# Making a modulation's sums for two channel tiles in a row, with a sixth slab buffer and the loads one slab further ahead

## The chip, the cores and the metric

The kernel runs on one core of one Trainium2 chip. The metric is the device time of one execution, in microseconds (us), as the median of several runs. Names used below: TensorE (PE) multiplies matrices and loads its weights (PEld), VectorE (DVE) and ScalarE (ACT) work on elements, GpSimd (POOL) does little here, and SyncE (SP) issues the transfers (DMA) from the device memory into the on-chip buffers. TensorE writes its results into banks of an accumulation memory, PSUM, from which VectorE and ScalarE read them.

## What is computed

One step of a backbone with one layer, for 128 context tokens and 256 latent tokens (384 in all), 2048 channels wide. The whole layer has two sub-layers, a mixer and a feed-forward part, each between two normalisations, and six vectors per condition that shift, scale and gate them. What the change touches is the first of these:

```
mod = silu(cond) @ w_ada + b_ada            # 6 vectors of 2048 channels, per condition
sh1, sc1, ga1, sh2, sc2, ga2 = split(mod, 6)
h = rmsnorm(x, norm_pre_mix) * (1.0 + sc1) + sh1
proj = h @ w_in                             # q, k, v, gates, low-rank factors, Fourier groups
```

There are two conditions, one for the context tokens and one for the latent ones. The vectors `sh1` and `sc1` come first, since nothing of the mixer can begin before h. The rest (attention with gates, a Fourier branch, their merge, the feed-forward part) follows and is not touched.

## The kernel before, in words

Everything is held with channels on the 128 partitions: x is 16 channel tiles of 128 channels by 384 tokens. Products in full precision are made of three passes over a high and a low half: a weight block is loaded (`raw`), ScalarE casts it to its high half (`whi`), VectorE subtracts to get the low half (`wlo`), and TensorE multiplies high by high, high by low and low by high.

The first stage is a loop over the 16 channel tiles, `for kb in range(KT)` at line 456. For tile kb it needs shift and scale for the 128 channels of that tile. These are a product of the two condition vectors with 2048 x 256 elements of the weights, kept as a "slab" of 2 MB: two buffers of 1 MB, loaded by `load_slab` (line 321). `gemv` (line 375) makes the sums: 16 matmuls over the 16 blocks of K, each with a stationary block of 32 columns, dealt out in turn to four groups of 32 partitions of the bank `pgm` (half `pgv`). The sums, spread over four groups, are copied by ScalarE (`ev`, line 490), transposed by TensorE into the other half (`pmod`, line 496), and reduced by VectorE (line 504), which then makes scale and shift (lines 507 and 511) and the modulated tile (line 513). ScalarE casts that to the high half of h (line 283), VectorE makes the low half (line 284).

In the same turn TensorE works on the tile before, kb-1: `vprod` (line 387) adds its part to all of v in six banks, in three passes of six matmuls, and `xprod` (line 411) makes two blocks of 128 columns in a single bank `px`, which VectorE adds up after each (line 409). In tiles 6, 10 and 14 a low-rank product (`lrprod`, line 421) comes in as well. For these products each tile loads a weight of 512 KB for v (`raw`, line 195) and a small one of 128 KB (`xraw`, line 331), each with two buffers; `split_w` (line 333) casts both, and the low halves are made by VectorE at the end of the turn, the large one at line 224, the small one at line 345.

The order on TensorE, ScalarE, VectorE and GpSimd is that of the program, written out by hand. In a plain turn TensorE does: the sums of kb; first xprod of kb-1; vprod pass 0; two transposes; second xprod; vprod pass 1; vprod pass 2. In tiles 1 and 2 (`wait`) a vprod pass and the first xprod come ahead of the sums. SyncE issues all transfers from one queue in the order of the program; an issue waits until its buffer is free. In turn kb it issues slab kb+1 (five half-slab buffers in all), the weight kb+1 and the small weight kb+1; in turn 4 five small loads follow (lines 362 to 366).

Of the kernel before, what the change touches and what calls it, by code (L numbers as in the profile page):

```python
# [11 lines left out]
F32 = mybir.dt.float32  # L12
# [8 lines left out]
P = 128  # L21
D = 2048
KT = D // P
# [73 lines left out]
def tile_step(ctx: ExitStack, tc: tile.TileContext, a, o):  # L97
    nc = tc.nc
    PE, ACT, DVE, POOL, SP = nc.tensor, nc.scalar, nc.vector, nc.gpsimd, nc.sync
# [9 lines left out]
    spad = const.tile([P, KT, 32], F32, name="spad")  # L109
# [5 lines left out]
    ident = const.tile([P, P], F32, name="ident")  # L115
# [23 lines left out]
    def halves(t):  # L139
        tl = [actp.tile([P, 8, T], F32, tag=f"{t}_{n}", name=f"{t}{n}") for n in ("hi", "lo")]  # L140
        return lambda k: tl[k // 8][:, k % 8, :], tl
# [48 lines left out]
    def load(raw=None):  # L190
        n, src = next(srcs, (0, None))
        if src is not None:
            if raw is None:
                raw = wp.tile([P, G], F32, tag="raw", name="raw", bufs=2)
            SP.dma_start(raw, src)
            raws.append((raw, n in folded))
# [85 lines left out]
    def split_act(hi, lo, src):  # L282
        ACT.copy(hi, src)
        DVE.tensor_sub(lo, src, hi.bitcast(F32))  # L284
# [31 lines left out]
    with ExitStack() as s:  # L316
        pa = s.enter_context(tc.tile_pool(name="pa", bufs=1))
        pb = s.enter_context(tc.tile_pool(name="pb", bufs=2))
        slabs = {}

        def load_slab(kb):
            slabs[kb] = [pb.tile([P, KT // 2, 256], F32, tag="slab", name="slab", bufs=5) for _ in range(2)]
            for n, sl in enumerate(slabs[kb]):
                SP.dma_start(sl, a["w_ada1"][kb, :, n * (KT // 2) : (n + 1) * (KT // 2), :])

# [2 lines left out]
        def load_w(kb):  # L328
            load()
            xraw[kb] = pb.tile([P, XU * P], F32, tag="xraw", name="xraw", bufs=2)  # L330
            SP.dma_start(xraw[kb], a["w_x"][kb])
# [17 lines left out]
        for q in range(4):  # L349
            SP.dma_start(  # L350
                xnt[q // 2][:, 4 * (q % 2) : 4 * (q % 2) + 4, :], a["xT"][:, 4 * q : 4 * q + 4, :],
            )
        load_slab(0)
        SP.dma_start(cols, a["b_ada"])
        SP.dma_start(norms, a["norms"])
        load_w(0)
        load_slab(1)
        load_w(1)
        wlr = pa.tile([P, KT, 32], F32, name="wlr")

        def load_later():
            SP.dma_start(wlr, a["w_lr"])
            SP.dma_start(coef[:, 0:2], a["consts"][:, C_COEF : C_COEF + 2])
            SP.dma_start(bgate, a["b_gate"])
            SP.dma_start(gnorm, a["gnorm"])
            SP.dma_start(selr, a["consts"][:, C_SELR : C_SELR + 64])
# [2 lines left out]
        pv = [psm.tile([P, 512], F32, tag="mm", name="pv") for _ in range(3)]  # L369
        pv += [pss.tile([P, 512], F32, tag="side", name="pv") for _ in range(3)]  # L370
        pgm = pss.tile([P, 512], F32, tag="side", name="pgm")
        pgv, pmod = pgm[:, 0:256], pgm[:, 256:512]
        px = pss.tile([P, T], F32, tag="side", name="px")

        def gemv(kb, ks=range(KT)):
            slab = slabs[kb]
            for k in ks:
                q = 32 * (k % 4)
                PE.matmul(  # L379
                    pgv[q : q + 32, :], spad[:, k, :], slab[k // (KT // 2)][:, k % (KT // 2), :],  # L380
                    start=k < 4, stop=k >= KT - 4,
                )

# [3 lines left out]
        def vprod(kb, w, parts, ts=range(3)):  # L387
            js = passes(w)
            tg = [(t, g) for t in ts for g in range(2)]
            if kb < KT - 1:  # L390
                order = [(j, t, g) for j in parts for t, g in tg]
            else:
                order = [(j, t, g) for t, g in tg for j in parts]
            for j, t, g in order:
                x_, w_ = js[j]
                PE.matmul(  # L396
                    pv[2 * t + g], hT[x_][:, kb, t * P : (t + 1) * P], w_[:, g * 512 : (g + 1) * 512],
                    start=kb == 0 and j == 0, stop=kb == KT - 1 and j == 2,
                )
# [11 lines left out]
        def xprod(u, kb, w):  # L411
            def mm():
                for j, (x_, w_) in enumerate(passes(w)):
                    PE.matmul(px, w_[:, u * P : (u + 1) * P], hT[x_][:, kb, :], start=j == 0, stop=j == 2)  # L414

            return mm, lambda dst=None: flush(xacc[u], kb == 0, dst)

        def lrprod(kb):
            def mm():
                for q in range(4):  # L420
                    PE.matmul(
                        px[32 * q : 32 * q + 32, :], wlr[:, kb + q, :], scr[:, (kb + q) % 8, :], start=True, stop=True,
                    )

            return mm, lambda dst=None: flush(lracc, kb == 0, dst)
# [20 lines left out]
        DVE.tensor_scalar_add(bsc1[:, 0, :], cols[:, 1, :], 1.0)  # L446
        DVE.tensor_scalar_add(bsc1[:, 1, :], cols[:, 4, :], 1.0)
        gemv(0, range(KT // 2, KT))
        ev = pb.tile([P, 256], F32, tag="ev", name="ev")
        ACT.copy(ev, pgv)  # L450
        for t in range(3):
            PE.matmul(px[:, t * P : (t + 1) * P], r0[:, t : t + 1].to_broadcast([P, P]), ident, start=True, stop=True)
        rstd = pa.tile([P, T], F32, name="rstdA")
# [1 line left out]
        prev = None  # L455
        for kb in range(KT):
            if kb and kb + 1 < KT:
                load_slab(kb + 1)
                load_w(kb + 1)
                if kb == 4:  # L460
                    load_later()

            wait = kb in (1, 2)
            if kb and not wait:
                gemv(kb)
            todo = []
            if kb > 4 and kb % 4 == 2:
                todo.append(lrprod(kb - 6))
            if kb:
                todo += [xprod(u, kb - 1, prev[1]) for u in range(XU)]  # L470
            todo += [None] * (4 - len(todo))
            flushes = [t[1] if t else lambda: None for t in todo]

            def pe_x(n):
                if todo[n]:
                    todo[n][0]()

            if wait:
                vprod(kb - 1, prev[0], (0,))
            pe_x(0)  # L480
            hf = scr[:, kb % 8, :]

            xr = hf if kb else qs[0]
            DVE.tensor_mul(xr, xn(kb), rstd if kb else px)
            flushes[0]()
            if wait:
                gemv(kb)
            if kb:
                ev = pb.tile([P, 256], F32, tag="ev", name="ev")
                ACT.copy(ev, pgv)  # L490
            lag = []
            new = split_w(kb, lag)
            if kb:
                vprod(kb - 1, prev[0], (1 if wait else 0,))
            for m in range(2):
                PE.transpose(pmod[:, m * P : (m + 1) * P], ev[:, m * P : (m + 1) * P], ident)
            if kb == 0:

                for _ in range(6):
                    PE.matmul(pv[5][:, 0:P], ones, ones, start=True, stop=True)  # L500
            pe_x(1)

            pm = pb.tile([P, 2, 2], F32, tag="pm", name="pm", bufs=2)
            DVE.tensor_reduce(
                pm, pmod.rearrange("p (m q r) -> p m r q", m=2, q=4)[:, :, 0:2, :], axis=mybir.AxisListType.X, op=ALU.add,
            )
            DVE.tensor_scalar(
                mods[:, 1, kb, :], pm[:, 1, :], bsc1[:, 0, kb : kb + 1], norms[:, 0, kb : kb + 1],
                op0=ALU.add, op1=ALU.mult,
            )  # L510
            DVE.tensor_scalar_add(mods[:, 0, kb, :], pm[:, 0, :], cols[:, 0, kb : kb + 1])
            for lo, hi, c in segs:
                DVE.tensor_scalar(
                    hf[:, lo:hi], xr[:, lo:hi], mods[:, 1, kb, c : c + 1], mods[:, 0, kb, c : c + 1],
                    op0=ALU.mult, op1=ALU.add,
                )
                if kb == 0:
                    ACT.activation(
                        hT[0][:, kb, lo:hi], xr[:, lo:hi], AF.Identity,
                        bias=mods[:, 0, kb, c : c + 1], scale=mods[:, 1, kb, c : c + 1],  # L520
                    )
            flushes[1]()
            if kb:
                split_act(hT[0][:, kb, :], hT[1][:, kb, :], hf)
            else:
                ACT.copy(rstd, px)
                DVE.tensor_sub(hT[1][:, kb, :], hf, hT[0][:, kb, :].bitcast(F32))
            if kb:
                if not wait:
                    vprod(kb - 1, prev[0], (1,))  # L530
                pe_x(2)
                flushes[2]()
            for sub in lag:
                sub()
            if kb:
                vprod(kb - 1, prev[0], (2,))
                pe_x(3)
                flushes[3]()
            prev = new
# [504 lines left out]
    mg32, _ = halves("B")  # L1044
    x1, x1t = halves("C")
    with ExitStack() as s:
# [49 lines left out]
        for i in range(KT):  # L1096
            p = psm.tile([P, T], F32, tag="mm", name="pmm")
            for g in range(2):
                n = 2 * i + g - 2 * KT
# [381 lines left out]
        n = 0  # L1481
# [100 lines left out]
        for kind, c, i in steps:  # L1582
# [8 lines left out]
            if kind == "D":  # L1591
                w = grab2()
                n, kh = i // 2, i % 2
                if kh == 0:
# [3 lines left out]
                    pool, tag = (pss, "side") if done % 2 or (c, n) == (NFC - 2, 3) else (psm, "mm")  # L1598
# [52 lines left out]
        n = d_order[-1]  # L1651
# [145 lines left out]
```

## Time and profile before

| | |
|---|---|
| median of 3 runs | 1960.13 us (1959.51 to 1961.31) |
| the profiled execution's own time | 1962.6 us |
| its span | 1960.3 us |
| PE busy | 1943.0 us (99%) |
| DVE busy | 1630.9 us (83%) |
| ACT busy | 908.6 us (46%) |
| first stage, tiles 0 to 15 | sums from 15.3 to 132.5 us, end at about 138 us |
| slab loads | 32 of 1 MB, 9.8 us from issue to landing in the median |

A row of a timeline has the start and the duration in us, the engine, the line, the operation, what is written from what, the form, and the count; in brackets stands how long the engine was idle before and what ended that. "SPq" rows are the issues of transfers, not the transfers. In a table by stretches each row gives a stretch in us, its length, then busy time and (number of instructions) of PE, PEld, DVE, ACT and POOL, the granted clock of TensorE as a share of full speed, the share of the DMA engines' time that was in use, and GB/s. A row of a tile gives the minimum, median and maximum duration in ns. Matmuls overlap one another, so a busy TensorE need not be at its peak: the distance from start to start tells what an instruction costs in a row of its kind.

### The profile page before, as it was taken

What the parts mean: (1) busy time and instruction counts of PE and PEld (TensorE: products, weight loads), DVE (VectorE), ACT (ScalarE), POOL (GpSimd) and SP (SyncE); (2) the same over time, 40 slices, a digit from 0 to 9 for tenths busy, and PEclk for the clock granted to TensorE, in tenths of its full rate; (3) what the DMA queues carried; (4) which work ended last, traced back from release to release, by engine and by line L of the source; (5) the groups of instructions that cost most, each with busy time, mean ns of one, the idle gap of its engine ahead of it and who ended that gap; (6) DMA issues with size and microseconds to landing.
All of it is one profiled execution on the core that took longest, in us unless ns stands there. A gap on an engine that the chain in (4) does not pass through costs nothing.

```text
span 1960.3 us, 27459 instructions
## 1 busy us (share of the span) xinstructions
PE 1943.0 (99%) x10544; PEld 1720.4 (88%) x10544; DVE 1630.9 (83%) x2091; ACT 908.6 (46%) x1281; POOL 32.2 (2%) x44
## 2 busy tenths in 40 slices
PE   8999999999999999999999999999999999999998
PEld 5679999999999999999988888888888888888886
DVE  5668788878767797977789998999898989887875
ACT  4233454544345654446455444444444444444444
POOL 0000000000000000004000000000000000000001
PEclk9999999999999999999999999999999999999999
DMA  9977677767755786755345445463536263626243
GB/s 389 373 259 268 220 257 238 233 218 246 246 189 158 224 268 217 233 183 206 111 148 172 161 133 170 140 196 121 193 123 208 94 213 108 202 74 193 74 157 134
DMA packets 189267, 380.05 MB, mean 194 GB/s; under 512 B 14029, under 2 KB 112525, under 8 KB 184785
## 3 DMA queue, kind: packets, MB, share of 16 engines
q1 hardware_dynamic: 188992, 377.92, 58.0%
q8 instruction: 82, 1.34, 0.3%
q14 instruction: 49, 0.39, 0.1%
q10 hardware_dynamic: 144, 0.39, 0.1%
HBM read 361.48 MB, written 16.78 MB: 193 GB/s over the span
## 4 chain that ended last, share of the span: by engine, by line
PE 87%; DMA 6%; issue 3%; DVE 3%; ACT 1%; POOL 0%; POOLq 0%; SPq 0%; ACTq 0%; DVEq 0%
PE pgu L1498 31%; PE pmm L257 30%; PE pdn L1498 16%; PE pv L396 2%; DMA slab<-in_w_ada 1%; PE pf L996 1%; DMA raw<-in_w_in 1%; PE pgm L379 1%; PE pmm L1252 1%; DVE wlo L224 1%; DVE adacc L572 1%; DMA raw<-in_w_out 1%; PE px L414 1%; PE ptr L1559 1%; ACT whi L223 1%
## 5 line engine op out<-in xcount | busy, mean ns | idle before, releaser
L257 PE MATMUL pmm<-A_hi,whi 128*128 128x384 f32 x1200 | 404.4, 337 | 0.0
L257 PE MATMUL pmm<-A_lo,whi 128*128 128x384 f32 x1200 | 401.5, 335 | 0.5 <-DVE A_lo L284 0.5
L257 PE MATMUL pmm<-A_hi,wlo 128*128 128x384 f32 x1200 | 401.4, 334 | 0.0
L1399 ACT CAST whi<-u 128x1024 fp32r<-128x1024 f32 x200 | 210.8, 1054 | 286.4 <-DVE u L1383 86.2
L223 ACT CAST whi<-raw 128x1024 fp32r<-128x1024 f32 x181 | 189.7, 1052 | 211.8 <-DMA raw<-in_w_gate 72.5
L1399 ACT CAST whi<-raw 128x1024 fp32r<-128x1024 f32 x175 | 184.3, 1053 | 197.8 <-PE pgu L1498 61.1
L224 DVE TENSOR_TENSOR wlo<-raw,whi 128x1024 fp32r<-128x1024 f32 x179 | 218.4, 1222 | 67.1 <-ACT whi L223 64.8
L1410 DVE TENSOR_TENSOR wlo<-u,whi 128x1024 fp32r<-128x1024 f32 x200 | 244.2, 1221 | 33.6 <-ACT whi L1399 18.4
L1498 PE MATMUL pgu<-whi,A_hi 128*128 128x512 f32 x640 | 250.0, 391 | 0.0
L1498 PE MATMUL pgu<-whi,A_lo 128*128 128x512 f32 x640 | 249.3, 389 | 0.0
L1410 DVE TENSOR_TENSOR wlo<-raw,whi 128x1024 fp32r<-128x1024 f32 x175 | 213.6, 1220 | 34.4 <-ACT whi L1399 25.1
L257 PEld LDWEIGHTS pmm<-A_hi,whi 128*128 128x128 f32 x1200 | 225.3, 188 | 2.9 <-issue 1.4
L257 PEld LDWEIGHTS pmm<-A_lo,whi 128*128 128x128 f32 x1200 | 225.4, 188 | 1.2 <-DVE A_lo L284 1.0
L257 PEld LDWEIGHTS pmm<-A_hi,wlo 128*128 128x128 f32 x1200 | 225.3, 188 | 0.0
L572 DVE SCALAR_TENSOR_TENSOR adacc<-adaw,spad,adacc 128x1024 f32<-128x1024 f32 x180 | 222.9, 1280 | 0.4
L1498 PE MATMUL pdn<-whi,hid_hi 128*128 128x512 f32 x480 | 186.9, 389 | 0.0
L1498 PE MATMUL pdn<-whi,hid_lo 128*128 128x512 f32 x480 | 186.8, 389 | 0.0
L1498 PE MATMUL pgu<-wlo,A_hi 128*128 128x512 f32 x640 | 184.2, 389 | 0.0
L1498 PEld LDWEIGHTS pgu<-whi,A_hi 128*128 128x128 f32 x640 | 120.1, 188 | 26.0 <-issue 0.8
L1498 PEld LDWEIGHTS pgu<-wlo,A_hi 128*128 128x128 f32 x640 | 120.2, 188 | 25.3
L1498 PEld LDWEIGHTS pgu<-whi,A_lo 128*128 128x128 f32 x640 | 120.2, 188 | 25.0
L1498 PE MATMUL pgu<-whi,S 128*128 128x512 f32 x480 | 131.1, 395 | 0.0
(369 smaller groups left out, 2759.2 us busy)
## 6 DMA issues: line engine op xcount, KB each, us to landing
adaw<-in_w_ada SPq DMA_DIRECT2D x96, 512.0 KB, 4.1
raw<-in_w_d SPq DMA_DIRECT2D x88, 512.0 KB, 3.7
slab<-in_w_ada SPq DMA_DIRECT2D x32, 1024.0 KB, 9.8
raw<-in_w_gate SPq DMA_DIRECT2D x64, 512.0 KB, 4.7
raw<-in_w_g SPq DMA_DIRECT2D x48, 512.0 KB, 3.3
raw<-in_w_u SPq DMA_DIRECT2D x48, 512.0 KB, 3.6
raw<-in_w_in SPq DMA_DIRECT2D x44, 512.0 KB, 4.4
u<-in_w_u SPq DMA_DIRECT2D x40, 512.0 KB, 4.8
```

What stands on the lines that cost most here:

```text
L223: ACT.copy(hi, raw)
L224: sub = lambda: eng.tensor_sub(lo, raw, hi.bitcast(F32))
L257: PE.matmul(dst, w[wi][:, k * n + n0 : k * n + n0 + P], x[xi][:, k0 + k, :], start=first and k == 0 and j == 0, stop=last and k == kts - 1 ...
L379: PE.matmul(pgv[q : q + 32, :], spad[:, k, :], slab[k // (KT // 2)][:, k % (KT // 2), :], start=k < 4, stop=k >= KT - 4,)
L396: PE.matmul(pv[2 * t + g], hT[x_][:, kb, t * P : (t + 1) * P], w_[:, g * 512 : (g + 1) * 512], start=kb == 0 and j == 0, stop=kb == KT - 1 ...
L414: PE.matmul(px, w_[:, u * P : (u + 1) * P], hT[x_][:, kb, :], start=j == 0, stop=j == 2)
L572: DVE.scalar_tensor_tensor(acc[:, c, :], w, spad[:, k, c : c + 1], acc[:, c, :], op0=ALU.mult, op1=ALU.add,)
L996: PE.matmul(pf[:, 0 : 2 * HT], w[0][:, c], x[k], start=k == 0, stop=False)
L1252: PE.matmul(hp[u], hw[u][j][:, ((k - 1) % 8) * P : ((k - 1) % 8 + 1) * P], h2[m][:, k - 1, :], start=k == 1 and j == m == 0, stop=k == KT ...
L1399: ACT.copy(hi, src)
L1410: DVE.tensor_sub(lo, src, hi.bitcast(F32))
L1498: PE.matmul(dst, stat[x_][m], mov(w[w_], m), start=first and w_ == m == x_ == 0, stop=last and w_ == m == 1,)
```

## The change

From the ninth tile on (kb = 8) the sums are made for two tiles in a row: in an even turn `gemv` runs for kb and for kb+1, the one into the first half of `pgm`, the other into the second; a single copy takes all 512 columns to `ev`, which now has one buffer of 512 columns instead of two of 256. In the odd turn there are no sums and no copy. The transposes of a tile go back into its own half of the bank. For that, slabs have six half-slab buffers, and the loads are further ahead: in turn 3 two slabs are issued, 4 and 5, the second after the weights of tile 4, and after that each turn kb issues slab kb+2 ahead of the weights of kb+1. The order of everything else is the same.

```diff
-            slabs[kb] = [pb.tile([P, KT // 2, 256], F32, tag="slab", name="slab", bufs=5) for _ in range(2)]
+            slabs[kb] = [pb.tile([P, KT // 2, 256], F32, tag="slab", name="slab", bufs=6) for _ in range(2)]
...
-        load_slab(0)
+        slab_order = iter(range(KT))
+
+        def next_slab():
+            kb = next(slab_order, None)
+            if kb is not None:
+                load_slab(kb)
+
+        next_slab()
...
-        load_slab(1)
+        next_slab()
...
-        pgv, pmod = pgm[:, 0:256], pgm[:, 256:512]
...
-        def gemv(kb, ks=range(KT)):
+        def gemv(kb, ks=range(KT), at=0):
...
-                    pgv[q : q + 32, :], spad[:, k, :], slab[k // (KT // 2)][:, k % (KT // 2), :],
+                    pgm[q : q + 32, at : at + 256], spad[:, k, :], slab[k // (KT // 2)][:, k % (KT // 2), :],
...
-        ev = pb.tile([P, 256], F32, tag="ev", name="ev")
-        ACT.copy(ev, pgv)
+        ev = pb.tile([P, 512], F32, tag="ev", name="ev", bufs=1)
+        ACT.copy(ev[:, 0:256], pgm[:, 0:256])
...
             if kb and kb + 1 < KT:
-                load_slab(kb + 1)
+                next_slab()
                 load_w(kb + 1)
+                if kb == 3:
+                    next_slab()
                 if kb == 4:
                     load_later()
...
-            if kb and not wait:
+
+            pair = kb >= 8
+            if pair and kb % 2 == 0:
+                for n in range(2):
+                    gemv(kb + n, at=256 * n)
+            elif kb and not wait and not pair:
                 gemv(kb)
...
-            if kb:
-                ev = pb.tile([P, 256], F32, tag="ev", name="ev")
-                ACT.copy(ev, pgv)
+            at = 256 * (kb % 2) if pair else 0
+            if kb and at == 0:
+                n = 512 if pair else 256
+                ev = pb.tile([P, 512], F32, tag="ev", name="ev", bufs=1)
+                ACT.copy(ev[:, 0:n], pgm[:, 0:n])
+            pmod = pgm[:, at : at + 256] if pair else pgm[:, 256:512]
...
-                PE.transpose(pmod[:, m * P : (m + 1) * P], ev[:, m * P : (m + 1) * P], ident)
+                PE.transpose(pmod[:, m * P : (m + 1) * P], ev[:, at + m * P : at + (m + 1) * P], ident)
```

## The prediction

> **What bounds the kernel now.** I read the page first (busy shares, slices, chain), then the table by stretches for the first stage alone, since the change touches nothing else, then the timelines of TensorE, VectorE and SyncE inside that stage.
>
> ```profile
> span 1960.3 us, 27459 instructions
> PE 1943.0 (99%) x10544; PEld 1720.4 (88%) x10544; DVE 1630.9 (83%) x2091; ACT 908.6 (46%) x1281; POOL 32.2 (2%) x44
> PE 87%; DMA 6%; issue 3%; DVE 3%; ACT 1%; POOL 0%; POOLq 0%; SPq 0%; ACTq 0%; DVEq 0%
> ...
> 40.00:51.00 11.00, 11.00 (x77) 8.42 (x76) 7.01 (x19) 3.31 (x7) 0.00 (x0) 1.00 1.01 409
> 59.40:76.40 17.00, 16.10 (x129) 11.01 (x132) 10.14 (x24) 4.38 (x8) 0.00 (x0) 1.00 1.03 413
> 76.40:138.00 61.60, 61.50 (x481) 43.93 (x480) 39.24 (x91) 18.07 (x33) 0.41 (x1) 1.00 0.81 304
> 138.00:1960.00 1822.00, 1811.15 (x9565) 1628.86 (x9564) 1547.37 (x1898) 862.01 (x1193) 30.47 (x34) 1.00 0.56 182
> ```
>
> TensorE ends the program: 99% busy, 87% of the chain, clock at 1.00 in each stretch (the column before the DMA share). The first stage runs to about 138 us and has two parts. Up to some 76 us the transfers are full (share 1.01 and 1.03 at 409 and 413 GB/s), and TensorE lacks 0.9 us of 17.0 in the second row. From 76.4 us, which is where tile 8 (the ninth) begins, the transfers have room (0.81) and TensorE is busy 61.50 of 61.60 us. So the lookahead acts in a stretch bound by transfers, the pairing in a stretch bound by TensorE, and what either gains or loses there goes through to the end: the stretch after it is 1811.15 of 1822.00 busy.
>
> **The change, part 1: two sums in a row from tile 8 on.** The four odd tiles 9, 11, 13, 15 lose their own block of sums; the even tile before makes both. No matmul goes away. What goes are changes between the 128x32 form of the sums and the 128x128 form of the products.
>
> ```profile
> 83.82 1.93 PE L379 MATMUL pgm<-slab,spad 128*32 128x256 f32 x32
> 85.68 0.44 PE L414 MATMUL px<-A_hi,whi 128*128 128x384 f32 x1
> 85.96 0.34 PE L414 MATMUL px<-A_hi,wlo 128*128 128x384 f32 x1
> ...
> 88.44 1.55 PE L396 MATMUL pv<-wlo,A_hi 128*128 128x512 f32 x6
> 89.83 1.53 PE L396 MATMUL pv<-whi,A_lo 128*128 128x512 f32 x6
> 91.28 1.93 PE L379 MATMUL pgm<-slab,spad 128*32 128x256 f32 x32
> ...
> 99.74 1.07 PE L379 MATMUL pgm<-slab,spad 128*32 128x256 f32 x16
> ...
> L379 PE MATMUL pgm<-slab,spad x512: 379/379/403, 15.3 to 132.1; 128*32 128x256 f32 x171
> ```
>
> Six products take 89.83 - 88.44 = 1.39 us where more of their kind follow and 91.28 - 89.83 = 1.45 where the sums follow: 0.06 for the change into the small form. From the first sum to the next product it is 85.68 - 83.82 = 1.86. So a block costs 1.92 us of TensorE's line. Inside it the 32 records start (1.93 - 0.38) / 31 = 0.05 apart, so a second block appended costs 32 x 0.05 = 1.60. Each pair saves 0.32 us; four pairs: **-1.3 us**. Four copies of the sums on ScalarE become part of the copies of the even tiles; ScalarE is busy 18.07 of 61.60 us there, so I cost the saving and the longer copy at nothing. The cover is the product block between sums and transposes (1.39 us and more).
>
> In the odd tiles the block was also cover. The first product after it (px) needs the low half of the small weight, which VectorE makes last (line 345).
>
> ```profile
> 84.25 0.42 DVE L345 TENSOR_TENSOR wlo<-xraw,whi 128x256 fp32r<-128x256 f32 x1
> ...
> 100.06 0.42 DVE L345 TENSOR_TENSOR wlo<-xraw,whi 128x256 fp32r<-128x256 f32 x1
> ...
> 29.97 0.42 DVE L345 TENSOR_TENSOR wlo<-xraw,whi 128x256 fp32r<-128x256 f32 x1
> ...
> 29.88 0.33 PE L414 MATMUL px<-A_hi,whi 128*128 128x384 f32 x1
> 30.45 0.44 PE L414 MATMUL px<-A_hi,wlo 128*128 128x384 f32 x1 [0.24 <-DVE wlo L345]
> ```
>
> Tile 2 already has this order, with no sums ahead of px, and shows the wait: the low half ends at 29.97 + 0.42 = 30.39 and the second px product starts at 30.45, 0.06 later. Apply that to tile 9. Without its sums px would start at 83.82 - 0.06 = 83.76, its second product 85.96 - 85.68 = 0.28 later, at 84.04; the low half ends at 84.25 + 0.42 = 84.67, so it starts at 84.73. Wait: 0.7 us. Tile 11: due 99.74 - 0.06 + 0.28 = 99.96, the low half ends 100.48, start 100.54: 0.6 us. Nothing in the change makes VectorE earlier there: its chain starts at the transposes, which move with TensorE. With 13 like 9 and 15 like 11: 2 x (0.7 + 0.6) = **+2.6 us**. Behind the waiting product stand the second product block, the transposes and VectorE's whole next chain, all of them moved by the same time. In the even tiles there is no such wait, since two blocks cover it. The two ends: 0 if VectorE had the low half ready, 2.8 at 0.7 each. I take 2.6, from the rows.
>
> **Part 2: loads a slab further ahead.** At tile 3 one slab more is issued, and from then on slab k+2 stands on SyncE's queue ahead of the weights of tile k+1.
>
> ```profile
> 39.49 1.59 SPq L324 DMA_DIRECT2D slab<-in_w_ada  x2
> 45.02 0.33 SPq L195 DMA_DIRECT2D raw<-in_w_v  x1
> ...
> 48.54 0.33 SPq L366 DMA_DIRECT2D selr<-in_consts  x1
> 51.08 1.68 SPq L324 DMA_DIRECT2D slab<-in_w_ada  x2
> 52.86 0.37 SPq L195 DMA_DIRECT2D raw<-in_w_v  x1
> ...
> DMA to landing us min/median/max: 7.3/7.3/7.3
> ...
> DMA to landing us min/median/max: 8.8/8.8/8.8
> ...
> 59.38 1.07 PE L379 MATMUL pgm<-slab,spad 128*32 128x256 f32 x16
> 61.31 1.07 PE L379 MATMUL pgm<-slab,spad 128*32 128x256 f32 x16 [0.86 <-DMA slab<-in_w_ada]
> 68.89 1.93 PE L379 MATMUL pgm<-slab,spad 128*32 128x256 f32 x32
> ```
>
> (The landings are those of the weight issued at 45.02 and of the second half slab of the pair at 51.08, issued at 52.43.) Slab 6 lands at 52.43 + 8.8 = 61.2, and tile 6 waits for it: it takes 68.89 - 59.38 = 9.51 us, tile 10 with the same work 99.74 - 91.28 = 8.46. With slab 6 issued right behind slab 5, at about 40.5, that wait of **-1.05 us** goes.
>
> What is late next is the weights. Weight 5 now lands at 45.02 + 7.3 = 52.3; with 2.1 MB of slab 6 ahead of it, at 410 GB/s, 5.1 us later: 57.4. Weight 6 now lands behind slab 6, at about 61.2 + 0.52 MB / 410 GB/s = 62.5, so 10.2 us after weight 5, with the small loads of line 362 to 366 and one slab between them. After the change the same set stands between them, with slab 7 for slab 6: 57.4 + 10.2 = 67.6 if the queue runs as unevenly as now, or, by bytes alone (some 3.1 MB at 410), 57.4 + 7.5 = 64.9. I take the middle, 66.2: SyncE still holds back the slab after the small loads, but later than now.
>
> When does that hurt? These rows are tile 6 on ScalarE and VectorE:
>
> ```profile
> 62.89 1.05 ACT L223 CAST whi<-raw 128x1024 fp32r<-128x1024 f32 x1
> 63.85 0.40 ACT L344 CAST whi<-xraw 128x256 fp32r<-128x256 f32 x1
> 66.31 0.51 ACT L283 CAST A_hi<-scr 128x384 fp32r<-128x384 f32 x1 [2.06 <-DVE scr L513]
> ...
> 69.22 0.42 DVE L345 TENSOR_TENSOR wlo<-xraw,whi 128x256 fp32r<-128x256 f32 x1
> ```
>
> The weight's high half starts at t, the small one's ends 63.85 + 0.40 - 62.89 = 1.36 later, then the cast of the products' left side, and from its start to the end of VectorE's last low half 69.64 - 66.31 = 3.33. So the low half is there at t + 4.69. Tile 7, now starting 1.05 earlier at 67.84, wants its second px product 1.86 + 0.28 later, at 69.98. So t up to 65.2 costs nothing (it is 62.89 now), and each us beyond costs one. At 66.2: **+1.0**; between 64.9 and 67.6: 0 to 2.4. Weight 5 at 57.4 costs nothing: tile 6 starts with its sums and the low-rank product, and has until after 62. Weight 7 comes 5.1 us later too, but from tile 7 on the queue needs about 6.7 us per tile (2.8 MB at 413) against TensorE's 91.28 - 83.82 = 7.46, so the debt shrinks. Slab 9, now wanted in tile 8: weight 6 at 66.2 plus 5.0 MB (two slabs, a weight, two small ones) in 12.1 us, 78.3; the last half of the second block is due at 67.84 + 1.0 + 7.46 + 1.9 + 0.8 = 79.0. It fits by 0.7; I take 0, at worst 1.
>
> The weight's lateness rests on the queue being served in order, as the 7.3 us of a 0.5 MB load behind 2.1 MB of slab show. The Trainium skill says so too: "DMA: Bandwidth & Descriptors", section "Queues, rings and completion order", has each DMA engine take its descriptors in ring order. By that rule the late weights stand; were the transfers shared out evenly instead, the small ones would pass the slab, part 2 would be -1.05 and the whole sum +0.25.
>
> **The sum.** -1.3 + 2.6 - 1.05 + 1.0 = **+1.25 us**. The profiled execution took 1962.6 us (span 1960.3 and 2.3 around it), which is 2.5 above the median of the three runs, 1960.13; the sum is made on its rows, and I put it on the median: 1961.4. Bounds: -1.3 + 0 - 1.05 + 0 = -2.35 to -1.3 + 2.8 - 1.05 + 2.4 + 1.0 = +3.85. For this kernel 0.2% is 3.9 us, about what a measurement can tell from no change, so the whole stretch between the bounds counts as no change.
>
> **The rivals.**
>
> *The pairing is clean.* VectorE's low half is no bar in the odd tiles, and the weights come in time: -2.35, 1957.8 us. For it: TensorE waits in the steady part now for almost nothing. Against it: tile 2's row shows that wait. Chance 0.20.
>
> *The weights choke (slower).* Weight 6 sits behind a slab more, and a fetch of instructions (82 packets in the page's row of that queue, below, on the same 16 engines) falls on it. With the other terms at +0.25 it passes 3.9 us when weight 6 lands after 65.2 + 3.65 = 68.9, which is 1.3 us beyond my upper value of 67.6. At 70, say, it costs 4.8 and the time is 1960.1 + 0.25 + 4.8 = 1965.2. For it: share 1.03 in that stretch, so nothing is made good at once. Against it: weight 6 may be 2.3 us later (65.2 for 62.89) than now for free. Chance 0.11.
>
> ```profile
> q8 instruction: 82, 1.34, 0.3%
> ...
> SPq L324 <- DMA slab<-in_w_ada: 2.1, 1, 2.1
> ```
>
> *The change of form is worth far more than its rows say (faster).* To pass -3.9 us with tile 6's 1.05, and the waits of the odd tiles gone as well, each pair must save 0.72 us instead of 0.32, that is, a second block for 1.2 us: 0.0375 per record instead of 0.05. No row shows that spacing. 1956.0 us. Chance 0.05.
>
> *It doesn't do what it says.* SyncE reaches the extra slab no earlier, because it waits for older landings, as it does for 2.1 us ahead of 51.08 (the row above, of SyncE's own waits); then tile 6 keeps its wait, the weights are not late, and only the pairing is left: -1.3 + 2.6 = +1.3, 1961.4, and slab 9 holds up tile 8. Chance 0.09, and the same time as the forecast.
>
> **How the numbers follow.** The forecast has 0.55, and its own range is 1960 to 1963. The range 1957.8 to 1964.0 runs between the two bounds. Slower by over 0.2%: 0.11 for the choked queue and 0.01, out of the forecast's, for an unseen wait. Faster: 0.05. Within 0.2%: 0.83.
>
> **What would show each step.** In the timeline after: 64 records of sums in one row at about 77 us, some 3.5 us long, the px products right behind; in tiles 9, 11, 13, 15 a wait of about 0.65 us at the second px product, put down to VectorE line 345. In tile 6, no wait for a slab. On ScalarE, waits for the weight in tiles 5 and 6 of about 3 and 4 us, and in tile 7 a wait of TensorE for line 345 of about 1 us. The end of the first stage comes about 1 us later, and the rest has the same length as now. I am wrong if TensorE waits for a slab in tile 8, if the weights are not late, or if anything after 138 us changes by more than a microsecond.

## The result and the profile after

The changed kernel takes 1963.43 us in the median of 20 runs (1962.52 to 1967.04), the kernel before 1960.65 us in 20 (1959.51 to 1961.87). The ratio is 1.0015, with a 95% interval of 1.0009 to 1.0021: slower by 1.8 to 4.1 us, and clear of no change, though within the 0.2% that the prediction counted as such. The time lies inside the wide predicted range (1957.8 to 1964.0) and 0.4 us above the forecast's own (1960 to 1963).

The profiled execution of after has a span of 1961.4 us, only 1.1 more than that of before. The spans mislead here, since what follows the first stage isn't equally long even in executions of one kernel: in three further ones of the kernel before (below), the rest of the span behind the stage took 1822.9, 1821.3 and 1824.1 us. So I measure the first stage alone, from the first sum of tile 4 to the low-rank product that follows tile 15. Before, these two rows bound it:

```profile
44.45 1.93 PE L379 MATMUL pgm<-slab,spad 128*32 128x256 f32 x32
...
138.06 0.85 PE L421 MATMUL px<-scr,wlr 128*32 128x384 f32 x8
```

It takes 138.06 - 44.45 = 93.61 us. In TensorE's timeline of after (the first row is cut short by the end of the stretch that was asked for):

```profile
44.57 0.85 PE L385 MATMUL pgm<-slab,spad 128*32 128x256 f32 x12
...
59.50 1.93 PE L385 MATMUL pgm<-slab,spad 128*32 128x256 f32 x32
...
67.96 1.93 PE L385 MATMUL pgm<-slab,spad 128*32 128x256 f32 x32
69.82 0.44 PE L420 MATMUL px<-A_hi,whi 128*128 128x384 f32 x1
70.76 0.44 PE L420 MATMUL px<-A_hi,wlo 128*128 128x384 f32 x1 [0.50 <-DVE wlo L345]
...
76.19 3.90 PE L385 MATMUL pgm<-slab,spad 128*32 128x256 f32 x64
...
85.54 0.33 PE L420 MATMUL px<-A_hi,whi 128*128 128x384 f32 x1
86.53 0.44 PE L420 MATMUL px<-A_hi,wlo 128*128 128x384 f32 x1 [0.66 <-DVE wlo L345]
86.81 0.34 PE L420 MATMUL px<-A_lo,whi 128*128 128x384 f32 x1
...
102.04 0.33 PE L420 MATMUL px<-A_hi,whi 128*128 128x384 f32 x1
102.93 0.44 PE L420 MATMUL px<-A_hi,wlo 128*128 128x384 f32 x1 [0.56 <-DVE wlo L345]
...
108.38 3.66 PE L385 MATMUL pgm<-slab,spad 128*32 128x256 f32 x64
111.97 0.44 PE L420 MATMUL px<-A_hi,whi 128*128 128x384 f32 x1
...
140.31 0.85 PE L427 MATMUL px<-scr,wlr 128*32 128x384 f32 x8
```

The stage takes 140.31 - 44.57 = 95.74 us. Tile 6 has lost its wait (67.96 - 59.50 = 8.46 us), tile 7 has gained one (76.19 - 67.96 = 8.23, and 7.46 without), the pairs stand in rows of 64, and the odd tiles wait at the second small product for line 345. The sums of waits and the stretch of the paired tiles say it in one row each (the second: stretch, length, PE busy first):

```profile
PE px L420 <- DVE wlo L345: 2.4, 4, 0.7
...
76.20:140.30 64.10, 61.54 (x481) 44.39 (x480) 39.38 (x91) 18.05 (x29) 0.41 (x1) 1.00 0.75 291
```

TensorE counts as busy as long as before in these eight tiles (61.54 us against 61.50), but the stretch has grown from 61.6 to 64.1. The equal busy time doesn't mean that the pairing saved nothing: the rows below put its saving at 1.3 us, and about 1.1 us of slower starts around the four waits, which count as busy, take most of it back. On ScalarE the weights are late by what was forecast:

```profile
57.42 1.05 ACT L223 CAST whi<-raw 128x1024 fp32r<-128x1024 f32 x1 [2.95 <-DMA raw<-in_w_v]
...
66.41 1.05 ACT L223 CAST whi<-raw 128x1024 fp32r<-128x1024 f32 x1 [4.48 <-DMA raw<-in_w_v]
```

Forecast were 57.4 for weight 5 and 66.2 for weight 6.

### The profile page after: what moved, and what is told of

It reads as the page before. It is cut to its first block, busy times and chain, and to the rows that moved or that the text cites. A ratio compares the mean times of both kernels' runs of the same rounds, so it can differ in the third digit from the quotient of the medians.

```text
span 1961.4 us, 27440 instructions
## 1 busy us (share of the span) xinstructions
PE 1942.8 (99%) x10544; PEld 1721.5 (88%) x10544; DVE 1630.5 (83%) x2091; ACT 908.5 (46%) x1277; POOL 32.2 (2%) x44
## 4 chain that ended last, share of the span: by engine, by line
PE 89%; DMA 4%; issue 3%; DVE 2%; ACT 1%; POOL 0%; SPq 0%; POOLq 0%; ACTq 0%; DVEq 0%
PE pmm L257 33%; PE pgu L1514 31%; PE pdn L1514 16%; PE pv L402 2%; DMA raw<-in_w_v 1%; PE pmm L1268 1%; PE pgm L385 1%; DMA slab<-in_w_ada 1%; DVE wlo L224 1%; PE pf L1012 1%; PE ptr L1575 1%; PE px L420 1%; DMA xraw<-in_w_x 1%; PE po L661 1%; DMA raw<-in_w_in 0%
## 5 line engine op out<-in xcount | busy, mean ns | idle before, releaser
L224 DVE TENSOR_TENSOR wlo<-raw,whi 128x1024 fp32r<-128x1024 f32 x179 | 218.3, 1221 | 64.1 <-ACT whi L223 63.5
```

The costliest lines, as they stand in the source:

```text
L224: sub = lambda: eng.tensor_sub(lo, raw, hi.bitcast(F32))
```

## The experiments

The measure of all of them is the same length of the first stage, since most of their times lie within 2 us of the kernel before and the intervals of the ratios are about as wide. It is read from one execution of each. Five (the lookahead from turn 5, the weights first, and the three further ones of the kernel before) were run only once, so they have no ratio.

### Was the gain in tile 6 there to be had?

```diff
 e4_small_loads_later (on the kernel before)
                 load_slab(kb + 1)
+                if kb == 5:
+                    load_later()
                 load_w(kb + 1)
-                if kb == 4:
-                    load_later()
```

> The kernel before with one move: the five small loads are issued behind slab 6 instead of ahead of it. No sixth buffer, no pairing. Theory (slab 6 was late because its issue stood behind the small loads, which wait for landings): slab 6 is issued at about 46 us instead of 51, lands by 58, tile 6 waits no longer, and the weights stay in time: -1.05 us, 1959.6 us. Rival (the transfers were simply full, so that slab 6 could not land sooner): tile 6 keeps its wait, no change.

Tile 6 took 67.94 - 59.48 = 8.46 us, the stage 137.12 - 44.55 = 92.57, a microsecond less than in the profile before; the ratio is 0.9997 (0.9988 to 1.0006). Taken alone, that looks like the theory. It was a run meant for something else, the lookahead moved from turn 3 to turn 5, that put it in doubt:

```diff
 e6_lookahead_from_5 (on the changed kernel)
-                if kb == 3:
+                if kb == 5:
                     next_slab()
```

> The changed kernel with the extra slab issued in turn 5 instead of 3. Theory (the order of slab and weight on the queue decides): tile 6 has its wait for slab 6 again (+1.05 us), weight 6 comes in time and tile 7 has no wait (-0.8), weight 7 is late instead but the two blocks of tile 8 cover that; slab 9 lands at about 79.5 us against 79 wanted. The stage ends 0.2 to 0.8 us later than with the change. Rival (tile 7's wait comes from the pairing or from VectorE and not from the weights): tile 7 keeps its wait, the stage ends 1.05 us later.

Slab 6 was issued where the kernel before issues it, and tile 6 had no wait all the same (59.38 to 67.83, 8.45 us): the forecast of this run missed there. Tile 7 had none either, as the theory said (67.83 to 75.30), and TensorE waited 0.64 us for slab 9. The stage took 95.58 us. So the kernel before was profiled three times more, unchanged.

> The kernel before, profiled once more. The run with the lookahead from turn 5 kept slab 6 where it was and yet showed no wait in tile 6. Theory A (that wait belongs to the order of the loads): tile 6 takes 9.5 us again. Theory B (it depends on when a fetch of instructions falls on the queue in one execution): tile 6 takes 8.5 us in some executions, slab 6 lands near 60 us there, and the first stage is a microsecond shorter than in the profile before.

> The kernel before, another execution. Theory A: tile 6 takes 9.5 us. Theory B: 8.5 to 9.5 us, with the time of the fetch near 56 or 57 us.

> The kernel before, another execution. Theory A: tile 6 takes 9.5 us. Theory B: 8.5 to 9.5 us, with the time of the fetch near 56 or 57 us.

Theory A is out, and the times that theory B gives came in all three. TensorE's rows, two each:

```profile
59.53 1.93 PE L379 MATMUL pgm<-slab,spad 128*32 128x256 f32 x32
67.98 1.93 PE L379 MATMUL pgm<-slab,spad 128*32 128x256 f32 x32
```

```profile
59.44 1.93 PE L379 MATMUL pgm<-slab,spad 128*32 128x256 f32 x32
67.89 1.93 PE L379 MATMUL pgm<-slab,spad 128*32 128x256 f32 x32
```

```profile
59.53 1.93 PE L379 MATMUL pgm<-slab,spad 128*32 128x256 f32 x32
67.99 1.93 PE L379 MATMUL pgm<-slab,spad 128*32 128x256 f32 x32
```

Tile 6 takes 8.45 us in each, and the stage 92.56, 92.57 and 92.58 us, as with the small loads moved, which therefore gained nothing. The wait of 0.86 us was in one execution of four. In that one, slab 6's second half took 8.8 us to land; in the three it took 7.7, 7.4 and 7.8 (in the second from 52.67 to 60.1, in time for the 60.45 at which the profile before wanted it). A fetch of instructions falls at another time there. The queue's row in the stretch from 54 to 56 us of that run, and in the one from 56 to 58 us of the profile before (none from 54 to 56):

```profile
q8 instruction: 1, 0.02, 2.8%
...
DMA to landing us min/median/max: 7.4/7.4/7.4
```

```profile
q8 instruction: 1, 0.02, 3.0%
```

The other two have it from 54 to 56 us as well. The transfers as a whole were no slower: from 54 to 60 us they moved 362 GB/s in the profile before and 358, 360 and 368 in the three. That the fetch causes the late landing is what the times suggest; nothing here moved it on purpose, so the cause of the late landing stays open.

The time of a whole execution doesn't tell whether it holds this wait: the three without it took 1962.13, 1960.51 and 1963.52 us, the one with it 1962.6.

The kernel before, then, has a stage of 92.57 us in most executions, and the changed one is 95.74 - 92.57 = 3.2 us longer in its stage, which agrees with the 1.8 to 4.1 us of the medians.

### The two parts apart

```diff
 e1_lookahead_alone (on the changed kernel)
-            pair = kb >= 8
+            pair = False
```

> Part 2 alone: sixth buffer and loads a slab ahead, no tile paired. Theory (the sum of parts): tile 6 loses its wait for slab 6 (-1.05 us), tile 7 gets a wait for the low half of the small weight, put down to line 345, because weight 6 lands behind slab 7 (+0.8, as after the change); the first stage ends 0.2 to 0.4 us earlier than before, 1960.3 us against 1960.6. Rival (the loss of the change sits in the late weights): 2 us or more slower than before already here.

The stage took 137.30 - 44.29 = 93.01 us, 0.4 more than the kernel before has in most executions; tile 7 took 75.58 - 67.68 = 7.90 us with a wait for line 345. Ratio 0.9998 (0.9990 to 1.0007). In this execution the lookahead alone costs those 0.4 us and gains nothing. The rival, a loss of 2 us from late weights, is out.

### What the odd tiles wait for

Two cures for the same wait, one on VectorE, one on TensorE.

```diff
 e2_small_low_first (on the changed kernel)
-            for sub in lag:
+            for sub in lag[::-1] if pair and kb % 2 == 0 else lag:
                 sub()
```

> The changed kernel with one order on VectorE turned: in the even paired tiles the low half of the small weight is made ahead of that of the large one. Theory (odd tiles wait for VectorE's last low half): that half is ready 1.1 us sooner, so the waits of 0.6 to 0.7 us in tiles 9, 11, 13, 15 go, with some 0.1 us each of restart: the stage ends about 3.0 us earlier than with the change, 1960.4 us against 1963.4, level with before. Rival (TensorE restarts slowly there for another reason, or another wait is just behind): under 1 us gained.

VectorE's rows of the end of tile 8, and TensorE's of the start of tile 9 (the third is the next pair), in that run:

```profile
84.54 0.42 DVE L345 TENSOR_TENSOR wlo<-xraw,whi 128x256 fp32r<-128x256 f32 x1
84.87 1.22 DVE L224 TENSOR_TENSOR wlo<-raw,whi 128x1024 fp32r<-128x1024 f32 x1
...
85.16 0.33 PE L420 MATMUL px<-A_hi,whi 128*128 128x384 f32 x1
85.33 0.34 PE L420 MATMUL px<-A_hi,wlo 128*128 128x384 f32 x1
85.51 0.34 PE L420 MATMUL px<-A_lo,whi 128*128 128x384 f32 x1
...
90.66 3.66 PE L385 MATMUL pgm<-slab,spad 128*32 128x256 f32 x64
```

The small low half is ready at 84.96 and the second product starts 0.17 us behind the first, without a wait. The stage took 136.44 - 44.47 = 91.97 us: 3.8 less than with the change, 0.6 less than before (the 92.57 us). Forecast were 3.0 less than with the change. The median is 1960.27 us, ratio to before 0.9992 (0.9983 to 1.0001).

This run also gives the price of the wait and the worth of the pairing. Tiles 10 and 11 took 106.27 - 90.66 = 15.61 us where the profile before has 107.20 - 91.28 = 15.92; tiles 12 and 13 0.36 us less, 14 and 15 0.33 less: 0.33 us gained per pair. And since the products run 0.17 apart when they are let, the wait in tile 9 is not 0.66 us but 86.53 - 85.54 - 0.17 = 0.82, in tile 11 102.93 - 102.04 - 0.17 = 0.72, and the product behind it follows after 0.28 us instead of 0.17, 0.11 more. Four of them: 2 x (0.93 + 0.83) = 3.5 us.

```diff
 e3_pass_ahead (on the changed kernel)
+            odd = pair and kb % 2 == 1
-            if wait:
+            if wait or odd:
                 vprod(kb - 1, prev[0], (0,))
...
-                vprod(kb - 1, prev[0], (1 if wait else 0,))
+                vprod(kb - 1, prev[0], (1 if wait or odd else 0,))
...
-                if not wait:
+                if not (wait or odd):
                     vprod(kb - 1, prev[0], (1,))
```

> The changed kernel with the order of tile 2 in the odd paired tiles on TensorE: product pass 0 of v ahead of the first small product, pass 1 ahead of the transposes. VectorE's order is as in the changed kernel. Theory: 1.4 us of products cover the 0.7 us, the four waits go, about 3.0 us earlier than with the change, 1960.4 us, as in the run that turns VectorE's order. Rival: the transposes come 1.4 us later in the turn, so that VectorE's chain ends later and the wait reappears in the even tile after: no gain.

The waits in the odd tiles are gone here as well (the small products of tile 9 start at 87.12, 87.29 and 87.47), and the rival's wait in the even tiles did not come. The stage took 137.09 - 44.40 = 92.69 us, 3.05 less than with the change; that it isn't as short as the other is tile 7, whose wait was longer in this execution (76.66 - 67.80 = 8.86 us). Ratio to before 1.0000 (0.9991 to 1.0009). But a wait for VectorE does come, just behind the stretch that is measured:

```profile
138.90 0.50 PE L402 MATMUL pv<-wlo,A_hi 128*128 128x512 f32 x1 [0.53 <-DVE wlo L224]
```

Here the second product behind the low-rank product starts 138.90 - 137.09 = 1.81 us after it, in the profile after 141.43 - 140.31 = 1.12. So 0.7 of the 3.05 us is paid again behind tile 15: the rival's wait shows up behind the last tile, and by these rows turning VectorE's order is the better cure.

So the wait is one for VectorE's last low half, and it can be taken away from either side.

### What the order of the loads decides

```diff
 e7_weights_first (on the changed kernel)
-                next_slab()
+                if kb < 4:
+                    next_slab()
                 load_w(kb + 1)
-                if kb == 3:
+                if kb >= 3:
                     next_slab()
```

> The changed kernel with each turn's weights issued ahead of its slab, so that slab k+2 stands behind weight k+1. Theory: weights in time, tiles 6 and 7 without a wait, but slab 9 stands behind weight 8, whose issue waits for VectorE at about 68 us, and lands at about 81; the last half of tile 8's second block is due at about 78, so TensorE waits 2 to 3 us for a slab in tile 8. The stage ends 1 to 2 us later than with the change. Rival (six buffers are enough for pairing, whatever the order): no wait for a slab in tile 8, 0.8 us earlier than the change.

Tiles 6 and 7 had no wait (59.66 to 68.11 to 75.58); the pairs waited for slabs:

```profile
79.97 1.07 PE L385 MATMUL pgm<-slab,spad 128*32 128x256 f32 x16 [1.44 <-DMA slab<-in_w_ada]
...
128.54 1.07 PE L385 MATMUL pgm<-slab,spad 128*32 128x256 f32 x16 [0.87 <-DMA slab<-in_w_ada]
```

1.44 us in tile 8 where 2 to 3 were forecast, and 0.87 us in tile 14, which was not. The stage took 97.64 us, 1.9 more than with the change, as forecast. Six buffers alone are not enough when pairing starts at tile 8; with the extra slab issued in turn 3, as in the change, the weights are late in tile 7 instead.

### The change once more, and the cures together

> The changed kernel once more, on the chip of the other runs of this set. Theory: the four waits in the odd tiles are the same to 0.05 us (they are VectorE's fixed chain), those in tiles 7 and 8 differ by some tenths of a us, since they hang on landings; 2 to 3 us slower than before. Rival (the loss is chance in the landings): the waits in the odd tiles vary as well.

```profile
79.11 1.07 PE L385 MATMUL pgm<-slab,spad 128*32 128x256 f32 x16 [0.96 <-DMA slab<-in_w_ada]
86.61 0.45 PE L420 MATMUL px<-A_hi,wlo 128*128 128x384 f32 x1 [0.66 <-DVE wlo L345]
```

The same kernel as in the profile after, without an edit. The four waits in the odd tiles are the same to the hundredth (0.66, 0.56, 0.66, 0.56). Tile 7 took 75.35 - 67.52 = 7.83 us instead of 8.23, and TensorE waited 0.96 us for slab 9 instead of about 0.2. The stage took 96.31 us, the median was 1963.77 us, the ratio 1.0014 (1.0005 to 1.0023).

```diff
 e5_paired_from_10 (on the changed kernel)
                 next_slab()
+                if kb == 5:
+                    load_later()
                 load_w(kb + 1)
-                if kb == 3:
+                if kb == 8:
                     next_slab()
-                if kb == 4:
-                    load_later()
...
-            pair = kb >= 8
+            pair = kb >= 10
...
-            for sub in lag:
+            for sub in lag[::-1] if pair and kb % 2 == 0 else lag:
```

> The cures put together: small loads behind slab 6, the slab ahead only from tile 8 on (behind its weights), tiles paired from the eleventh (10/11, 12/13, 14/15), and in the even paired tiles the small weight's low half made first. Theory: tile 6 -1.05 us, tile 7 without a wait, each of three pairs -0.3 as in the run with VectorE's order turned: the stage ends 1.7 to 1.95 us earlier than before, some 1959 us; a wait of up to 0.3 us for slab 11 may be left in tile 10. Rival (the lookahead brings late weights wherever it starts): a wait of ScalarE for weights in tiles 8 to 10 that comes out on TensorE, and no more than 1 us gained.

Nothing in the stage shows a wait of TensorE from tile 6 on, and tiles 10 and 11 take 106.08 - 90.47 = 15.61 us. The stage took 136.27 - 44.68 = 91.59 us, the shortest of all: 2.0 below the profile before, and 1.0 below the 92.57 of its other executions, which is three pairs at 0.33. The median is 1959.54 us against 1961.08 on its chip, ratio 0.9992 (0.9983 to 1.0001). The interval holds 1, so the gain is shown by the rows of the stage and not by the time of the whole kernel.

## Why the prediction was right, and where it was not

The sign of the sum was right, and the time stayed inside the wide range. The size was not: 1.25 us were forecast, the medians are 1963.43 - 1960.65 = 2.8 apart, and the stage is 3.2 longer. Two terms carry most of that: tile 6's gain was no property of the kernel (1.05), and the waits in the odd tiles were sized too small (0.9). Term by term:

- **Each pair saves 0.32 us: right in size, not by its working.** 0.33 was measured where nothing waits. The second block costs more than the forecast's 1.60: (111.97 - 108.38) - 1.86 = 1.73 us. The 32 records start in groups of four, eight groups 0.216 us apart, and I had spread them evenly over 31 gaps, though the prediction's own rows tell it: a row of 32 takes 1.93 us and one of 16 takes 1.07, so 16 more cost 0.86 and 32 more 1.72. Against that, the small products behind a block of products run 0.17 us apart and not 0.28.
- **A wait of 0.6 to 0.7 us in tiles 9, 11, 13 and 15: the mechanism, place and pattern right, 2.6 us forecast, 3.5 measured.** I moved the 0.28 between two products, which belongs to a change of form, into an order where there is none, and left out the 0.11 us by which the product behind a wait is slower.
- **Tile 6 gains 1.05 us: wrong.** Its wait was in the one execution that I read, not in three others of the same kernel. The step that failed is "tile 6 waits for it", taken from one row as what the order of the loads does. Another execution would have told; the 2.5 us by which that one stood above the median would not, since executions without the wait are as long.
- **The weights are late and tile 7 waits: right.** Weight 6 was cast from 66.41 where 66.2 was forecast. That it came so near is in part luck: 66.2 was the middle of two workings, 64.9 and 67.6, and in the four other runs with this order of loads (the change again, the lookahead alone, the two cures for the odd tiles) the cast started between 65.56 and 66.89. Tile 7's wait was 0.8 and 0.4 us in the two executions of the changed kernel and 0.3 to 1.4 in all five; 1.0 was forecast, 0 to 2.4 its bounds.
- **Slab 9 fits by 0.7 us: wrong.** The prediction names a wait for a slab in tile 8 as a sign of being wrong, and it came. TensorE waited about 0.2 us for it in one execution, and 0.96 in another, whose tiles 8 and 9 took 92.05 - 75.35 = 16.70 us against 124.01 - 108.48 = 15.53 for tiles 12 and 13, 1.2 longer; 1 was the bound. This wait trades with tile 7's: where the rows show the block's last quarter start after a wait, it is at 78.64 (VectorE's order turned), 78.73 (lookahead from turn 5, no wait in tile 7) and 79.11 us (the change again), so a shorter wait in tile 7 is in part given back in tile 8.
- **Nothing after 138 us changes by more than a microsecond: too narrow a sign.** The rest behind the stage took 1960.3 - 138.06 = 1822.2 us before and 1961.4 - 140.31 = 1821.1 after, 1.1 less; but three executions of the kernel before differ there by 2.8 us, so this says nothing about the change.

With what was measured: -1.3 + 3.5 + 0 + 0.8 + 0.2 = 3.2 us, and the stage is 95.74 - 92.57 = 3.17 longer. For the second execution -1.3 + 3.5 + 0 + 0.4 + 1.2 = 3.8, and it is 96.31 - 92.57 = 3.74. The rivals: the clean pairing was real as a mechanism, but needed VectorE's order turned; the choke did not come (weight 6 stayed 2.5 us below the 68.9 from which it would have decided); the form's change was worth no more than its rows said.

## What to carry to other kernels

A block of work that is moved away from an engine takes its cover along: look at what the engine meets next, find a place in the trace where that order already exists, and take the wait from there. A wait for a transfer in a single execution is not yet a property of the kernel: profile the kernel again before a gain is built on it, and don't go by the length of the execution. And where loads share one queue in order, one buffer loaded earlier makes those behind it later by its bytes: for weight 5, the next on the queue, bytes gave 57.4 us and it was cast from 57.42. Further down the queue it is less sure: for weight 6 bytes alone gave 64.9, and it was 66.41.

## What the runs showed of the hardware

A fetch of instructions (one packet of 0.02 MB in the rows above) falls at 54 to 56 us in three executions of the kernel before and at 56 to 58 us in one, so its place varies from one execution to the next. In that one, slab 6's second half landed at 61.2 us instead of 60.1 to 60.3, about 1 us later. I had put such a meeting into the slow rival as a chance; it may already have struck in the profile before, which isn't shown.

The matmuls of the sums, with 32 stationary columns each and dealt out to four groups, start four at a time, and each further four come 0.216 us later; a mean over their records hides that. And a small product that follows one that had waited starts 0.28 us after it (86.81 - 86.53), where it is 0.17 in a row without a wait (85.33 - 85.16).
